# Experts with at most 32 tokens: four 32-column tiles by branch, in a one-core flow-block kernel

## Chip, cores and metric

The kernel runs on one core of a Trainium2 chip. The metric is the device time of one execution in microseconds; before the change it is 1284.41 us (median of 3 runs, 1284.01 to 1285.48).

## What is computed

One block over 256 latent tokens of width 1024 (with 256 context tokens beside them): three token mixers, their merge, and then a mixture of experts, which is what the change touches.

```
def moe_ffn(h, w_router, b_router, w_gate_up, b_gate_up, w_down, b_down):
    logits = (h @ w_router + b_router).astype(jnp.float32)
    top_val, top_idx = lax.top_k(logits, TOP_K)              # 4 of 32
    probs = jax.nn.softmax(top_val, axis=-1)
    combine = jnp.einsum('nk,nke->en', probs, jax.nn.one_hot(top_idx, N_EXPERTS, ...))
    def expert(acc, xs):
        wgu, bgu, wd, bd, cw = xs                            # 1024x2048, 1024x1024
        gate, up = jnp.split(h @ wgu + bgu, 2, axis=-1)
        gate = jnp.minimum(gate, SWIGLU_LIMIT)
        up = jnp.clip(up, -SWIGLU_LIMIT, SWIGLU_LIMIT)
        glu = gate * jax.nn.sigmoid(SWIGLU_ALPHA * gate)
        return acc + cw[:, None] * (((up + 1) * glu) @ wd + bd), None
```

All is float32. The routing gives the 32 experts, in order, 17, 34, 33, 47, 48, 4, 19, 77, 8, 46, 101, 48, 28, 12, 11, 40, 25, 1, 46, 42, 36, 8, 28, 31, 44, 14, 21, 64, 12, 39, 32 and 8 tokens for the inputs used here.

## The kernel before

The mixers, the merge and the routing take the first 310 us. Then a loop in Python (line 1479 on) lays out the 32 experts one after another; the text calls them 0 to 31. The loop is unrolled: every expert has its own instructions on every engine.

**Tokens.** For an expert, `select` (L1358) makes a 0/1 table of its first 64 tokens (`SLOTS`), and `gather` (L1362) turns it into `hT`, the tokens' columns with the features on the 128 partitions, by matmuls against the normalized tokens `h2`; ScalarE applies scale and shift. Gathering is done for two experts at a time.

**Matmuls.** The weights are the moving operand. `gate_up` (L1388, matmul at L1392) loads 64 token columns of `hT` as the stationary operand and streams 512 weight columns past them; two such tiles (q = 0 and 1) stand side by side in the array, each with its own 512 of the 1024 columns, and write the upper and lower 64 partitions of one PSUM bank. Each matmul is float32 and runs as two passes, so the trace shows two records for each. An expert has a first half of `gate_up` (8 steps of 128 features), a second one, and `down` (L1410, matmul at L1414) of the same size. `biases` (L1385) opens each bank with one matmul that puts the bias there.

**Between them.** `act` (L1395) is the clamped SwiGLU on VectorE with one sigmoid on ScalarE. `turn` (L1403) transposes its result on TensorE and copies it to `gT`, the stationary operand of `down`. `spots` (L1373) makes the weighted scatter table, `spread` (L1416) multiplies the output of `down` by routing weight and gate, and `scatter` (L1421) adds it to four PSUM banks by 8 matmuls; an expert's `scatter` is issued within the next expert, after that one's first `gate_up`.

**More than 64 tokens.** Two `tc.If(tv > SLOTS)` per expert (L1503 and L1518) hold `rest_gate` (L1429) and `rest` (L1446), which do tokens 64 to 127 of the same expert with the same weights. TensorE, VectorE and ScalarE each load the expert's count into a register and take the branch by themselves. Experts 7 and 10 enter it. A last `tc.If` (L1557) for over 128 tokens is passed over.

**Weights.** SyncE issues all weight transfers from one list in the order of use (`pump`, L148; the transfer at L161). An expert has six of 2 MB: four for `gate_up` (two per half) and two for `down`; the last expert's `down` comes in four of 1 MB. Nine buffers of 2 MB take them in turn. `done` (key) frees a buffer in the program behind its last reader and issues the next transfer in the list, which waits on the chip until that reader has run.

**Order.** The order of instructions is that of the Python text (a manual schedule); there is no planner.

Of the kernel before, what the change touches and what calls it, by code (L numbers as in the profile page):

```python
# [16 lines left out]
AF = mybir.ActivationFunctionType  # L17
ALU = mybir.AluOpType
# [99 lines left out]
def kernel(ctx, tc, x, cx, cols, rows, csts, wsm, wgt, bada, brt, sgub, bdn, bgu,  # L118
# [45 lines left out]
    def weight(key):  # L164
        if key not in loaded:
            pump()
        return loaded[key][0]
# [6 lines left out]
    def halves(*key):  # L174

        w = weight(key)
        return [w[:, 0:2048], w[:, 2048:4096]]
# [47 lines left out]
    with ExitStack() as p1:  # L225
# [1058 lines left out]
        bsel = Buf(A2, NE, 2)  # L1284
# [20 lines left out]
        G.memset(bsel[:], 0.0)  # L1305
        for r in range(4):
            S.copy(out=bsel[32 * r:32 * r + 32, :, r % 2], in_=ident[32 * r:32 * r + 32, 32 * r:32 * r + 32])
# [15 lines left out]
    def sps2():  # L1323
        sbank.append(sbank.pop(0))
        return sbank[-1]
# [15 lines left out]
    for t in range(2):  # L1341
        mm(ps[0:1, 64:64 + NE], ones[:, 0:1], sel[:, t], start=t == 0, stop=t == 1)

# [10 lines left out]
    sw = ysum[:, 0:256].rearrange("p (t a n) -> p t a n", t=2, a=2)  # L1354
# [18 lines left out]
    def spots(b, sl, e):  # L1373
        for t in range(2):
            V.tensor_scalar_mul(sw[:, t], sl[:, t, :].unsqueeze(1).to_broadcast([P, 2, SLOTS]), cw[:, t, e:e + 1])
        pw = sps2()
        for t in range(2):
            T.transpose(pw[:, P * t:P * t + P], sw[:, t].rearrange("p a n -> p (a n)"), ident[:])  # L1378
        V.tensor_scalar(out=b["sT"][:], in0=pw[:, 0:256], scalar1=0.0, scalar2=None, op0=ALU.is_gt)  # L1379
        V.reduce_sum(out=b["cwv"][:, 0:1], in_=pw[:, 0:256], axis=AX.X)  # L1380

    def bias_of(e):
        V.tensor_copy(out=bse[e % 2][:].rearrange("p (q n) -> p q n", q=2), in_=bsel[:, e, :].unsqueeze(2).to_broadcast([P, 2, SLOTS]))  # L1383
# [11 lines left out]
    def act(b, hf, pg):  # L1395
        gc = b["gc"][hf]
        V.tensor_scalar_min(gc[:], pg[:, 0:256], LIMIT)  # L1397
        S.activation(out=sg[:], in_=gc[:], func=AF.Sigmoid, scale=SW_ALPHA)  # L1398
        V.tensor_scalar(out=up[:], in0=pg[:, 256:512], scalar1=LIMIT, scalar2=-LIMIT, op0=ALU.min, op1=ALU.max)
        V.tensor_tensor(out=gc[:], in0=gc[:], in1=sg[:], op=ALU.mult)  # L1400
        V.scalar_tensor_tensor(out=gc[:], in0=up[:], scalar=1.0, in1=gc[:], op0=ALU.add, op1=ALU.mult)

    def turn(b, hf):  # L1403
        pt = sps2()
        for j in range(2):
# [4 lines left out]
    def down(b, py, ks, w):  # L1410
        for k in ks:
            wk = w[k // 2].rearrange("p (k n) -> p k n", k=2)
            for q in range(2):
                mm(py[64 * q:64 * q + 64, :], b["gT"][:, k, :], wk[:, k % 2, 512 * q:512 * q + 512], start=k == 0, stop=k == KB - 1)  # L1414

    def spread(b, py):  # L1416
        V.scalar_tensor_tensor(out=ysum[:], in0=py[:], scalar=b["cwv"][:, 0:1], in1=g2q[:], op0=ALU.mult, op1=ALU.mult)  # L1417
        S.copy(out=yhx[:], in_=ysum[:])  # L1418
        V.tensor_tensor(out=ylx[:], in0=ysum[:], in1=yhx[:].bitcast(F32), op=ALU.subtract)
# [9 lines left out]
    def rest_gate(e, w):  # L1429

        gather(over, 0, 1)
        gather(over, 1, 1)
        pg = sps2()
        biases(e, 0, pg)
# [11 lines left out]
    def rest(e, g, wu, wd, end=False):  # L1446
        turn(over, 0)
        biases(e, 1, g)
# [19 lines left out]
    biases(0, 0, gbank[0])  # L1468
    V.tensor_copy(out=cnt[:, 0:NE], in_=ps[0:1, 64:64 + NE])
    V.reduce_max(out=cnt[:, NE:NE + 1], in_=ps[0:1, 64:64 + NE], axis=AX.X)  # L1470
    V.tensor_tensor(out=e4[:], in0=m8[:, :, 0:4], in1=m8[:, :, 0:1].to_broadcast([P, 2, 4]), op=ALU.subtract)
# [6 lines left out]
    eq.free()  # L1478
    for e in range(NE):
# [9 lines left out]
        gate_up(hT, g0, range(8), w)  # L1489
        act(cur, 0, g0)  # L1490
        if e:
            scatter(cur)
# [9 lines left out]
        over["hT"] = q_["hT"][:, 4:8].rearrange("p k (i j) n -> p (k i) j n", j=1)  # L1502
        with tc.If(tv > SLOTS):  # L1503
            rest_gate(e, w)
# [9 lines left out]
        if e < NE - 1:  # L1514
            wd = halves("dn", e, 0) + halves("dn", e, 1)
        else:
            wd = [weight(("dn1", e, i)) for i in range(4)]
        with tc.If(tv > SLOTS):  # L1518
            rest(e, g1, wu, wd)
# [9 lines left out]
        turn(cur, 1)  # L1529
        if e + 2 - e % 2 < NE:  # L1530
            gather(q_, e % 2, 2)
        if e + 1 < NE:
            biases(e + 1, 0, g1)
        down(cur, g0, range(4, 8), wd)
        for key in [("dn", e, 1)] if e < NE - 1 else [("dn1", e, 2), ("dn1", e, 3)]:
            done(key)
        if e < NE - 1:
            spread(cur, g0)
        else:
            ylast, lnb = Buf(A, 512), Buf(A, 2, D)  # L1540
            for i in range(2):
                S.dma_start(out=lnb[:, i, :], in_=lnr[2 + i:3 + i, :].to_broadcast([P, D]))
            V.scalar_tensor_tensor(out=ylast[:], in0=g0[:], scalar=cur["cwv"][:, 0:1], in1=g2q[:], op0=ALU.mult, op1=ALU.mult)
            scatter_whole(cur, ylast, True)
# [61 lines left out]
NR2 = 2840  # L1606
NA2S = 2
NA2 = 14592
# [14 lines left out]
def _layout(x, c, ctx, c_ctx, w_ada, b_ada, w_in, b_in, pool_w, pool_scale, qk_conv_w, qk_conv_b, mlstm_norm_g,  # L1623
# [31 lines left out]
    gu = gu.transpose(0, 5, 1, 3, 2, 6, 4, 7).reshape(NE, 4, 2, P, 2048).transpose(0, 1, 3, 2, 4).reshape(NE, 4, P, 4096)  # L1655
    dn = A(w_down)[0].reshape(NE, 2, 4, P, D).transpose(0, 1, 3, 2, 4).reshape(NE, 2, P, 4096)
    bg = A(b_gate_up)[0].reshape(NE, 2, 2, 2, 256).transpose(3, 0, 2, 1, 4).reshape(64, 2, 512)
# [23 lines left out]
```

## Time and profile before

| | |
|---|---|
| median of 3 runs | 1284.41 us |
| the profiled execution, whole | 1286.55 us |
| its span | 1284.7 us |
| mean granted TensorE clock | 0.984 |
| TensorE busy | 1189.9 us (93%) |
| VectorE busy | 461.2 us (36%) |
| ScalarE busy | 284.5 us (22%) |
| read from HBM | 468.92 MB, 366 GB/s over the span |

The whole time is what is compared; the span is the stretch that the profiler's rows cover, and all times in rows count from its start. PE is TensorE's matmuls and PEld its weight loads, which overlap them; a group of matmuls in a row that reads x32 holds 32 records, two for each float32 matmul of the program. Shares over the span mix the first 310 us with the expert loop, so the rows below are from single stretches.

### The profile page before, as it was taken

To read this page: it belongs to the slowest core of one execution; us is meant where nothing else is said; L and a number is where in the kernel's file an instruction comes from. 1 tells how busy PE (TensorE), PEld (TensorE's weight loads), DVE (VectorE), ACT (ScalarE), POOL (GpSimd) and SP (SyncE) were. 2 spreads that over 40 slices of the span, in tenths; PEclk is the share of its full clock that TensorE was granted. 3 is DMA by queue.
4 is the path that set the end of the run, shared out by engine and by line. 5 is a ranking of instruction groups with operands and counts; after the bars stand their busy time and mean duration, and the time that the engine had idled before them with its cause. 6 is when DMAs were issued, how large, how long until landed. Compare 5 with 4: busy or idle time off the path is not lost. (4 is left out here: it accounts for less than half of the span.)

```text
span 1284.7 us, 16504 instructions
## 1 busy us (share of the span) xinstructions
PE 1189.9 (93%) x6619; PEld 611.3 (48%) x6624; DVE 461.2 (36%) x988; ACT 284.5 (22%) x548; POOL 28.3 (2%) x42
## 2 busy tenths in 40 slices
PE   7997999999999999999999999999888999889884
PEld 5897889995333434334433334333333333333321
DVE  6488768796222222222212221222222122212223
ACT  5352745634111111111111111111111111111101
POOL 1000000002000000000000000000000000000000
PEclk9998999998999999999999999999999999999998
DMA  9745648777999999989959999999999999999993
GB/s 389 274 152 204 232 178 296 294 311 297 392 415 427 424 427 427 427 323 429 375 213 387 428 425 427 427 425 427 427 426 426 427 425 427 425 427 426 428 423 149
DMA packets 39470, 471.74 MB, mean 367 GB/s; under 512 B 4529, under 2 KB 4657, under 8 KB 7473
## 3 DMA queue, kind: packets, MB, share of 16 engines
q1 hardware_dynamic: 37008, 463.75, 87.3%
q10 hardware_dynamic: 1696, 4.40, 1.0%
q8 instruction: 89, 1.46, 0.5%
q0 software_dynamic: 640, 1.84, 0.5%
q14 instruction: 37, 0.30, 0.1%
HBM read 468.92 MB, written 1.05 MB: 366 GB/s over the span
## 5 line engine op out<-in xcount | busy, mean ns | idle before, releaser
L1392 PE MATMUL bank<-arena,arena 128*64 128x512 f32 x1808 | 408.8, 596 | 18.3 <-DMA arena<-in_wgu_dram 17.7
L1414 PE MATMUL bank<-arena,arena 128*64 128x512 f32 x1088 | 251.7, 604 | 25.5 <-DMA arena<-in_wdn_dram 17.9
L1392 PEld LDWEIGHTS bank<-arena,arena 128*64 128x64 f32 x1808 | 124.1, 137 | 260.5 <-issue 235.6
L1414 PEld LDWEIGHTS bank<-arena,arena 128*64 128x64 f32 x1088 | 79.3, 138 | 174.8 <-issue 152.7
L246 PE MATMUL bank<-rounded 128*128 128x256 f32 (+1 forms) x1152 | 149.6, 289 | 0.1
L246 PEld LDWEIGHTS bank<-rounded 128*128 128x128 f32 x1152 | 144.0, 195 | 1.8 <-issue 0.6
L1397 DVE TENSOR_SCALAR arena<-bank 128x256 f32<-128x256 f32 x68 | 28.9, 424 | 280.4 <-PE bank L1392 280.4
L1417 DVE SCALAR_TENSOR_TENSOR arena<-bank,arena,g2q 128x512 f32<-128x512 f32 x33 | 24.8, 751 | 271.8 <-PE bank L1414 163.3
L1398 ACT ACTIVATE arena<-arena 128x256 f32<-128x256 f32 x68 | 28.4, 417 | 366.5 <-DVE arena L1397 362.6
L1407 ACT COPY arena<-bank 128x256 f32<-128x256 f32 x68 | 25.3, 372 | 294.4 <-PE bank L1406 294.4
L1392 PE MATMUL bank<-arena 128*64 128x512 f32 x368 | 85.4, 606 | 3.0 <-DMA arena<-in_wgu_dram 2.6
L343 DVE TENSOR_TENSOR rounded<-arena,rounded 128x2048 fp32r<-128x2048 f32 x29 | 66.2, 2284 | 15.1 <-ACT rounded L338 15.1
L1367 PE MATMUL bank<-arena 128*128 128x128 f32 (+1 forms) x576 | 69.9, 275 | 0.7 <-DVE rounded L1383 0.7
L1367 PEld LDWEIGHTS bank<-arena 128*128 128x128 f32 x576 | 66.9, 192 | 1.5 <-ACT arena L1232 0.8
L1370 ACT ACTIVATE arena<-bank,shc 128x128 f32<-128x128 f32 (+1 forms) x144 | 53.3, 450 | 50.7 <-PE bank L1367 50.7
L338 ACT CAST rounded<-arena 128x2048 fp32r<-128x2048 f32 x29 | 55.0, 1898 | 9.2 <-PE bank L246 5.6
L1379 DVE TENSOR_SCALAR rounded<-bank 128x256 fp32r<-128x256 f32 x34 | 14.5, 425 | 117.0 <-PE bank L1378 117.0
L1392 PEld LDWEIGHTS bank<-arena 128*64 128x64 f32 x368 | 25.2, 139 | 53.6 <-issue 45.3
L1418 ACT CAST rounded<-arena 128x512 fp32r<-128x512 f32 x33 | 20.4, 618 | 111.5 <-DVE arena L1417 111.5
L1426 PE MATMUL bank<-rounded 64*128 64x512 f32 x264 | 40.8, 418 | 3.6 <-ACT rounded L1418 3.1
L1426 PEld LDWEIGHTS bank<-rounded 64*128 64x128 f32 x264 | 22.8, 184 | 33.9 <-issue 25.1
L1386 PE MATMUL bank<-rounded 128*128 128x512 f32 x68 | 32.5, 477 | 5.8 <-PEq L1503 3.8
(326 smaller groups left out, 889.5 us busy)
## 6 DMA issues: line engine op xcount, KB each, us to landing
arena<-in_wgu_dram SPq DMA_DIRECT2D x128, 2048.0 KB, 28.7
arena<-in_wdn_dram SPq DMA_DIRECT2D x62, 2048.0 KB, 27.3
arena<-in_win_dram SPq DMA_DIRECT2D x23, 1024.0 KB, 5.3
arena<-in_wada_dram SPq DMA_DIRECT2D x16, 1024.0 KB, 4.9
arena<-in_wad_dram SPq DMA_DIRECT2D x8, 1024.0 KB, 11.1
arena<-in_wbr_dram SPq DMA_DIRECT2D x4, 1024.0 KB, 5.6
arena<-in_wout_dram SPq DMA_DIRECT2D x4, 1024.0 KB, 5.5
arena<-in_wdn_dram SPq DMA_DIRECT2D x4, 1024.0 KB, 33.6
```

Of the source, the lines that this page charges most:

```text
L246: mm(o, l, r, start=start and n == 0, stop=stop and n == len(todo) - 1)
L338: S.copy(out=wh[:, 0:2048], in_=w)
L343: V.tensor_tensor(out=wl[:, 0:2048], in0=w, in1=wh[:, 0:2048].bitcast(F32), op=ALU.subtract)
L1367: mm(pg[:, w * k:w * k + w], h2[:, t, 512 * a + P * k:512 * a + P * k + P], b["sl"][:, t].rearrange("p i n -> p (i n)"), start=t == 0, sto ...
L1370: S.activation(out=b["hT"][:, 4 * a + k].rearrange("p i n -> p (i n)"), in_=pg[:, w * k:w * k + w], func=AF.Identity, scale=shc[:, 1, 4 * ...
L1386: mm(pg[:], bse[e % 2][:], bst[:, hf, :], start=True, stop=False, skip_group_check=True)
L1392: mm(pg[64 * q:64 * q + 64, :], hT[:, k, :], wk[:, k % 2, 512 * q:512 * q + 512], start=False, stop=k == KB - 1, skip_group_check=True)
L1397: V.tensor_scalar_min(gc[:], pg[:, 0:256], LIMIT)
L1398: S.activation(out=sg[:], in_=gc[:], func=AF.Sigmoid, scale=SW_ALPHA)
L1407: S.copy(out=b["gT"][:, 4 * hf:4 * hf + 4, :].rearrange("p (q j) n -> p j q n", q=2), in_=pt[:, 0:256].rearrange("p (j q n) -> p j q n", j ...
L1414: mm(py[64 * q:64 * q + 64, :], b["gT"][:, k, :], wk[:, k % 2, 512 * q:512 * q + 512], start=k == 0, stop=k == KB - 1)
L1426: mm(acc[t][hf][:], b["sT"][sl, P * t:P * t + P], y_[sl, :], start=False, stop=last and y_ is ylx, skip_group_check=True)
```

## The change

Experts 1 to 31 with at most `SMALL` = 32 tokens take a second copy of their code. In it the stationary tile has 32 token columns, four such tiles stand side by side, and each streams 256 weight columns, a quarter of the 1024. `act` then works on 128x128 elements rather than 128x256, `turn` needs one transpose rather than two, and `spread` multiplies the quarter results by a masked gate (`g2m`) and writes them twice, so that `scatter` stays as it is. The columns of the weights are permuted in HBM so that either form finds gate and up columns where it needs them, and the bias goes in by two matmuls (512 and 256 columns; the second table, `bsel2`, is zero for large experts).

The choice is made three times per expert, by `by_count`: a first part (first `gate_up`, `act`, `scatter`, and for the large copy the nested `rest_gate`), a second (second `gate_up`, `spots`, `turn`, `act`, nested `rest`) and a third (`down`, `turn`, `gather` for a later expert, its `biases`, `spread`). Expert 0 has the large copy alone. `done` now stands behind a whole part: the two `down` buffers are freed in the text after the third part. Ahead of the loop come eight small matmuls that put the counts on 128 partitions, four more copies on ScalarE, five VectorE steps and two memsets.

```
...
+    for r in range(4):
+        for t in range(2):
+            mm(ps[32 * r:32 * r + 32, 128:129], sel[:, t], ones[:, 0:1], start=t == 0, stop=t == 1)
...
-    def biases(e, hf, pg):
+    def biases(e, hf, pg, large=False):
         mm(pg[:], bse[e % 2][:], bst[:, hf, :], start=True, stop=False, skip_group_check=True)
+        if not large:
+            mm(pg[:, 0:256], bsb[e % 2][:], bst[:, hf, 256:512], start=False, stop=False, skip_group_check=True)
-    def gate_up(hT, pg, ks, w):
+    def gate_up(hT, pg, ks, w, small=False):
+        n, m = (4, SMALL) if small else (2, SLOTS)
+        c = D // n
         for k in ks:
             wk = w[k // 2].rearrange("p (k n) -> p k n", k=2)
-            for q in range(2):
-                mm(pg[64 * q:64 * q + 64, :], hT[:, k, :], wk[:, k % 2, 512 * q:512 * q + 512], start=False, stop=k == KB - 1,
+            for q in range(n):
+                mm(pg[m * q:m * q + m, 0:c], hT[:, k, 0:m], wk[:, k % 2, c * q:c * q + c], start=False, stop=k == KB - 1,
                    skip_group_check=True)
...
+        def by_count(part):
+
+            if e == 0:
+                part(False)
+                return
+            with tc.If(tv > SMALL) as cmp:
+                part(False)
+            with cmp.Else():
+                part(True)
+
+        def part_a(small):
+            gate_up(hT, g0, range(8), w, small)
+            act(cur, 0, g0, small)
+            if e:
+                scatter(cur)
+            if not small:
+                with tc.If(tv > SLOTS):
+                    rest_gate(e, w)
+
+        def part_b(small):
+            gate_up(hT, g1, range(4), wu, small)
+            spots(cur, p["sl"][:, :, e % 2, :], e, small)
+            turn(cur, 0, small)
+            gate_up(hT, g1, range(4, 8), wu, small)
+            act(cur, 1, g1, small)
+            if not small:
+                with tc.If(tv > SLOTS):
+                    rest(e, g1, wu, wd)
+
+        def part_c(small):
+            down(cur, g0, range(4), wd, small)
+            turn(cur, 1, small)
+            if e + 2 - e % 2 < NE:
+                gather(q_, e % 2, 2)
+            if e + 1 < NE:
+                biases(e + 1, 0, g1)
+            down(cur, g0, range(4, 8), wd, small)
+            spread(cur, g0, small, ylast if e == NE - 1 else None)
+
+        by_count(part_a)
...
         for i in range(2):
             done(("gu", e, i))
-        wu = halves("gu", e, 2) + halves("gu", e, 3)
-        biases(e, 1, g1)
-        gate_up(hT, g1, range(4), wu)
-        spots(cur, p["sl"][:, :, e % 2, :], e)
-        turn(cur, 0)
-        gate_up(hT, g1, range(4, 8), wu)
-        act(cur, 1, g1)
...
-        with tc.If(tv > SLOTS):
-            rest(e, g1, wu, wd)
+        biases(e, 1, g1, e == 0)
+        by_count(part_b)
         for i in range(2, 4):
             done(("gu", e, i))
...
-        down(cur, g0, range(4), wd)
-        for key in [("dn", e, 0)] if e < NE - 1 else [("dn1", e, 0), ("dn1", e, 1)]:
+        by_count(part_c)
+        for key in [("dn", e, i) for i in range(2)] if e < NE - 1 else [("dn1", e, i) for i in range(4)]:
             done(key)
...
-NR2 = 2840
+NR2 = 3096
+SMALL = 32
...
```

How the instructions stand on TensorE now, at two places of expert 1. The first is from the end of the nested `rest_gate` to the second `gate_up`; in the names, `bank_...` is a PSUM bank, `arena_2892` holds `hT` and `gT`, `arena_2574` and `arena` weights, `rounded_2891` the bias and scatter tables, and a form like 64x512 is stationary columns by streamed columns. Before:

```order
L1378 MATMUL bank_98<-ident,arena_2892 128x128 x2
L1392 MATMUL bank_97<-arena,arena_2892 64x512 x4
L1503 UNCONDITIONAL_BRANCH x2
L1386 MATMUL bank_101<-rounded_2891 128x512
L1392 MATMUL bank_101<-arena,arena_2892 64x512 x8
```

And with the change:

```order
L1411 MATMUL bank_97<-arena,arena_2892 64x512 x4
L1551 UNCONDITIONAL_BRANCH x2
L1411 MATMUL bank_99<-arena_2892 32x256 x16
L1411 MATMUL bank_99<-arena,arena_2892 32x256 x16
L1460 MATMUL bank_96<-rounded_2891 128x512 x2
L1460 MATMUL bank_94<-rounded_2891 128x512 x2
L1460 MATMUL bank_100<-rounded_2891 128x512 x2
L1460 MATMUL bank_95<-rounded_2891 128x512 x2
L1540 UNCONDITIONAL_BRANCH
L1401 MATMUL bank_101<-rounded_2891 128x512
L1403 MATMUL bank_101<-rounded_2891 128x256
L1540 COMPARE_AND_BRANCH
```

Behind the large copy with its nested branch stands the small one: 32 matmuls of 32x256 for `gate_up`, and the 8 of `scatter` once more. The bias has a second matmul, and a compare stands ahead of the second part.

The second place is from the end of the second part to `down`. Before:

```order
L1426 MATMUL bank_95<-rounded_2891 128x512 x2
L1518 UNCONDITIONAL_BRANCH x2
L1414 MATMUL bank_99<-arena,arena_2892 64x512 x8
L1406 MATMUL bank_98<-ident,arena_2892 128x128 x2
L1367 MATMUL bank_97<-arena_2892 128x128 x8
L1386 MATMUL bank_101<-rounded_2891 128x512
L1414 MATMUL bank_99<-arena_2574,arena_2892 64x512 x8
```

And with the change:

```order
L1427 MATMUL bank_97<-ident,arena_2892 128x128
L1411 MATMUL bank_101<-arena,arena_2892 32x256 x16
L1540 UNCONDITIONAL_BRANCH
L1540 COMPARE_AND_BRANCH
L1441 MATMUL bank_99<-arena,arena_2892 64x512 x8
L1431 MATMUL bank_98<-ident,arena_2892 128x128 x2
L1377 MATMUL bank_97<-arena_2892 128x128 x8
L1401 MATMUL bank_101<-rounded_2891 128x512
L1403 MATMUL bank_101<-rounded_2891 128x256
L1441 MATMUL bank_99<-arena_2574,arena_2892 64x512 x8
L1540 UNCONDITIONAL_BRANCH
L1441 MATMUL bank_99<-arena,arena_2892 32x256 x16
```

A compare of the count now stands ahead of `down`, and the whole third part, the `gather` for a later expert and the next bias among it, is there twice, once in each copy.

## Rows read from the trace of the kernel before

**Rows 1.** The page's 40 slices: what the DMA engines moved.

```profile
GB/s 389 274 152 204 232 178 296 294 311 297 392 415 427 424 427 427 427 323 429 375 213 387 428 425 427 427 425 427 427 426 426 427 425 427 425 427 426 428 423 149
```

**Rows 2.** Stretches: busy us by engine (x instructions), granted clock, DMA share, GB/s.

```profile
500.00:550.00 50.00, 47.25 (x235) 18.36 (x231) 12.11 (x30) 7.03 (x19) 0.00 (x0) 1.00 1.01 427
550.00:600.00 50.00, 49.38 (x249) 19.57 (x248) 11.14 (x28) 6.98 (x17) 0.00 (x0) 1.00 0.90 361
600.00:650.00 50.00, 49.13 (x250) 20.15 (x248) 11.86 (x31) 7.79 (x21) 0.00 (x0) 1.00 0.87 354
650.00:700.00 50.00, 47.27 (x227) 18.40 (x225) 10.35 (x25) 7.18 (x17) 0.00 (x0) 0.97 0.76 304
```

**Rows 3.** TensorE's timeline in expert 3: start, us, line, form, records [idle before].

```profile
397.19 7.04 PE L1392 MATMUL bank<-arena,arena 128*64 128x512 f32 x32
...
405.52 0.47 PE L1386 MATMUL bank<-rounded 128*128 128x512 f32 x1 [0.17 <-PEq L1503]
405.93 3.65 PE L1392 MATMUL bank<-arena,arena 128*64 128x512 f32 x16
...
423.52 1.03 PE L1392 MATMUL bank<-arena 128*64 128x512 f32 x4
```

**Rows 4.** TensorE's timeline: first stages of experts 21 and 31, and the next wait.

```profile
941.37 2.37 PE L1392 MATMUL bank<-arena,arena 128*64 128x512 f32 x10
...
1239.59 3.65 PE L1392 MATMUL bank<-arena 128*64 128x512 f32 x16 [1.14 <-DMA arena<-in_wgu_dram]
1244.49 1.51 PE L1392 MATMUL bank<-arena,arena 128*64 128x512 f32 x6 [1.25 <-DMA arena<-in_wgu_dram]
```

**Rows 5.** TensorE's timeline: first rows of experts 7, 8, 10 and 11.

```profile
502.57 3.60 PE L1392 MATMUL bank<-arena 128*64 128x512 f32 x16
...
559.66 1.03 PE L1392 MATMUL bank<-arena,arena 128*64 128x512 f32 x4
...
612.38 3.60 PE L1392 MATMUL bank<-arena 128*64 128x512 f32 x16
...
671.14 1.89 PE L1392 MATMUL bank<-arena,arena 128*64 128x512 f32 x8
```

**Rows 6.** SyncE's timeline, expert 7's first weights; the page's DMA issues.

```profile
467.03 0.38 SPq L161 DMA_DIRECT2D arena<-in_wgu_dram  x1
...
arena<-in_wgu_dram SPq DMA_DIRECT2D x128, 2048.0 KB, 28.7
```

**Rows 7.** Line 260: timeline, then its group (ns min/median/max).

```profile
47.53 0.59 PEld L260 LDWEIGHTS bank<-arena 128*32 128x32 f32 x16
47.53 1.07 PE L260 MATMUL bank<-arena 128*32 128x256 f32 x16
...
L260 PEld LDWEIGHTS bank<-arena x128: 106/110/178, 17.0 to 48.0; 128*32 128x32 f32 x128
```

**Rows 8.** TensorE's branch rows of lines 1503 and 1557 (ns min/median/max).

```profile
L1503 PEldq COMPARE_BRANCH  x34: 70/279/357, 316.8 to 1245.4; - x34
...
L1557 PEldq COMPARE_BRANCH  x1: 3752/3752/3752, 1267.3 to 1267.3; - x1
```

**Rows 9.** Timeline around the first `down` of expert 2.

```profile
387.73 2.79 PE L1414 MATMUL bank<-arena,arena 128*64 128x512 f32 x12 [0.31 <-PEq L1518]
...
387.99 0.42 ACT L1398 ACTIVATE arena<-arena 128x256 f32<-128x256 f32 x1 [3.74 <-DVE arena L1397]
```

**Rows 10.** The page: busy time by engine; queue of instruction reads (packets, MB, share).

```profile
PE 1189.9 (93%) x6619; PEld 611.3 (48%) x6624; DVE 461.2 (36%) x988; ACT 284.5 (22%) x548; POOL 28.3 (2%) x42
...
q8 instruction: 89, 1.46, 0.5%
```

**Rows 11.** ScalarE's timeline ahead of the loop.

```profile
307.09 0.90 ACT L1307 COPY arena<-ident 32x32 f32<-32x32 f32 x4
```

**Rows 12.** Stretches in expert 10: TensorE busy, granted clock, DMA share, GB/s.

```profile
655.00:658.00 3.00, 1.58 (x8) 1.00 0.58 246
661.00:664.00 3.00, 3.00 (x12) 0.58 0.00 0
```

More of the change, by code (lines that the diff above doesn't have):

```diff
@@ L1283 @@
         bse = [Buf(R, P) for _ in range(2)]
-        bsel = Buf(A2, NE, 2)
+        bsb = [Buf(R, P) for _ in range(2)]
+        bsel, bsel2 = Buf(A2, NE, 4), Buf(A2, NE, 4)
+        g2m = Buf(A2, 512)
+        few = Buf(A2, 2)
         alid = Buf(A2, P)
@@ L1305 @@
         G.memset(bsel[:], 0.0)
+        G.memset(bsel2[:], 0.0)
+        G.memset(g2m[:], 0.0)
         for r in range(4):
-            S.copy(out=bsel[32 * r:32 * r + 32, :, r % 2], in_=ident[32 * r:32 * r + 32, 32 * r:32 * r + 32])
+            rs = slice(32 * r, 32 * r + 32)
+            S.copy(out=bsel[rs, :, 2 * (r % 2):2 * (r % 2) + 2], in_=ident[rs, rs].unsqueeze(2).to_broadcast([32, NE, 2]))
+            S.copy(out=g2m[rs, 256 * (r % 2):256 * (r % 2) + 256], in_=g2q[rs, 256 * (r % 2):256 * (r % 2) + 256])
         G.tensor_tensor(out=bst[64:128], in0=bgr[64:128], in1=bst[64:128].bitcast(F32), op=ALU.subtract)
@@ L1403, in turn, with act @@
-    def turn(b, hf):
+    def act(b, hf, pg, small=False):
+        j = 1 if small else 2
+        gc, up_, sg_ = (z[:, 0:P * j].rearrange("p (j n) -> p j n", j=j) for z in (b["gc"][hf], up, sg))
+        pj = pg[:, 0:256 * j].rearrange("p (j a n) -> p j a n", j=j, a=2)
+        V.tensor_scalar_min(gc, pj[:, :, 0], LIMIT)
+        S.activation(out=sg_, in_=gc, func=AF.Sigmoid, scale=SW_ALPHA)
+        V.tensor_scalar(out=up_, in0=pj[:, :, 1], scalar1=LIMIT, scalar2=-LIMIT, op0=ALU.min, op1=ALU.max)
+        V.tensor_tensor(out=gc, in0=gc, in1=sg_, op=ALU.mult)
+        V.scalar_tensor_tensor(out=gc, in0=up_, scalar=1.0, in1=gc, op0=ALU.add, op1=ALU.mult)
@@ L1404, in turn @@
+    def turn(b, hf, small=False):
         pt = sps2()
+        if small:
+            T.transpose(pt[:, 0:P], b["gc"][hf][:, 0:P], ident[:])
+            S.copy(out=b["gT"][:, 4 * hf:4 * hf + 4, 0:SMALL], in_=pt[:, 0:P].rearrange("p (r n) -> p r n", r=4))
+            return
         for j in range(2):
@@ L1408, in turn, with down, spread @@
                in_=pt[:, 0:256].rearrange("p (j q n) -> p j q n", j=2, q=2))
-    def down(b, py, ks, w):
+    def down(b, py, ks, w, small=False):
+        n, m = (4, SMALL) if small else (2, SLOTS)
+        c = D // n
         for k in ks:
             wk = w[k // 2].rearrange("p (k n) -> p k n", k=2)
[L1413 to L1417, printed above, removed]
+            for q in range(n):
+                mm(py[m * q:m * q + m, 0:c], b["gT"][:, k, 0:m], wk[:, k % 2, c * q:c * q + c], start=k == 0, stop=k == KB - 1)
+    def spread(b, py, small=False, o=None):
+        y = o or ysum
+        if small:
+            V.scalar_tensor_tensor(out=y[:].rearrange("p (j n) -> p j n", j=2), in0=py[:, None, 0:256].to_broadcast([P, 2, 256]),
+                                   scalar=b["cwv"][:, 0:1], in1=g2m[:].rearrange("p (j n) -> p j n", j=2), op0=ALU.mult, op1=ALU.mult)
+        else:
+            V.scalar_tensor_tensor(out=y[:], in0=py[:], scalar=b["cwv"][:, 0:1], in1=g2q[:], op0=ALU.mult, op1=ALU.mult)
+        if o:
+            return
         S.copy(out=yhx[:], in_=ysum[:])
@@ L1467 @@
     bias_of(0)
-    biases(0, 0, gbank[0])
+    biases(0, 0, gbank[0], True)
     V.tensor_copy(out=cnt[:, 0:NE], in_=ps[0:1, 64:64 + NE])
     V.reduce_max(out=cnt[:, NE:NE + 1], in_=ps[0:1, 64:64 + NE], axis=AX.X)
+    V.tensor_scalar(out=few[:, 0:1], in0=ps[:, 128:129], scalar1=float(SMALL), scalar2=None, op0=ALU.is_le)
+    for q in range(2):
+        V.tensor_scalar_mul(bsel2[:, :, 2 * q + 1], bsel[:, :, 2 * q + 1], few[:, 0:1])
+        V.tensor_tensor(out=bsel[:, :, 2 * q + 1], in0=bsel[:, :, 2 * q + 1], in1=bsel2[:, :, 2 * q + 1], op=ALU.subtract)
     V.tensor_tensor(out=e4[:], in0=m8[:, :, 0:4], in1=m8[:, :, 0:1].to_broadcast([P, 2, 4]), op=ALU.subtract)
@@ L1488 @@
         g0, g1 = gbank if e % 2 == 0 else gbank[::-1]
[L1489 to L1492, printed above, removed]
+        wu = halves("gu", e, 2) + halves("gu", e, 3)
+        if e < NE - 1:
+            wd = halves("dn", e, 0) + halves("dn", e, 1)
+        else:
+            wd = [weight(("dn1", e, i)) for i in range(4)]
+        over["hT"] = q_["hT"][:, 4:8].rearrange("p k (i j) n -> p (k i) j n", j=1)
+        def by_count(part):
+            if e == 0:
+                part(False)
+                return
+            with tc.If(tv > SMALL) as cmp:
[29 more added lines that the diff above has]
+        by_count(part_a)
         if e == NE // 2:
```

53 lines of the change are left out of this document (16 added, 37 removed).

## The prediction

> **What bounds the kernel now.** I read the 40 slices first. From slice 12 on the transfers hold some 427 GB/s in nearly every slice, and sag around 550 to 700 us (323, 375 and 213 in slices 17, 19 and 20) [rows 1], while TensorE is busy 93% of the span [rows 10]. So both look like the bound, and the table of stretches is needed to tell which one is late where. In 500 to 550 us the transfers move 427 GB/s, in 550 to 600, 600 to 650 and 650 to 700 they move 361, 354 and 304 [rows 2]. Counted as idle transfer time that is (66 + 73 + 123) / 427 x 50 = 30.7 us, of which 66 / 427 x 50 = 7.7 lies before 600 us. The rest of the expert loop is carried by the weights: six 2 MB transfers per expert.
>
> Next, one expert on TensorE. Expert 3 runs from 397.19 to 423.52, so 26.33 us: 7.04 us for the first `gate_up`, and four blocks of 16 records at 3.65 (two for the second `gate_up`, two for `down`), together 21.64, and 4.69 of other work [rows 3]. Late in the loop every stage waits for its transfer: from 941.37 (first stage of expert 21) to 1239.59 (expert 31) lie 60 transfers in 298.22 us, 4.97 each, thus 29.8 us per expert [rows 4]. TensorE is therefore quicker than the weights by 3.5 us on an ordinary expert, and time saved on it is worth nothing there. It is the bound in two places only. Expert 7 takes 559.66 - 502.57 = 57.1 us and expert 10 takes 671.14 - 612.38 = 58.8 [rows 5], because they hold over 64 tokens and run the nested branches; buffers come free late, nine of them hold 9 x 4.97 = 44.7 us of transfers, and the stream stops. How long it stops depends on how far TensorE was already behind the weights when it got there. Expert 7's first weights were issued at 467.03 and need 28.7 us [rows 6], so they were there at 495.7, while TensorE began at 502.57: 6.9 us behind, and the idle time is 7.7. For expert 10 the same sum, 6.9 + (612.38 - 502.57) - 18 x 4.97 - 7.7, gives 19.6 us behind, and the idle time is 23.
>
> **The change, step by step.** By the reference's routing 16 of experts 1 to 31 have at most 32 tokens: 5, 6 and 8 before expert 10, and 13 after it. Experts 1 to 4 and 9 take the large path.
>
> *Small matmuls.* A stage has 32 records of 128x512 now (7.04 us) and gets 64 of 128x256. The trace holds that very form in line 260: 16 such records in 1.07 us, with 0.59 us of weight loads inside it [rows 7]. At worst 64 cost 64 / 16 x 1.07 = 4.28 us; without the run-out of a block of 16 nearer 3.5. Three stages: 10.5 to 12.9 us in place of 21.64. To the 4.69 of other work come two 256-column bias matmuls (half of 0.47 each [rows 3]), three jumps of some 0.3 [rows 8], and about 1 us in `part_c`, where half of `down` (now 1.8 us) covers less of the `act` that the next transposes wait for. A small expert takes 18 to 20 us; I take 19.
>
> *Large path.* It pays for the branches. The first `down` used to start at 387.73, while ScalarE's sigmoid of `act` began at 387.99 and takes 0.42 [rows 9]; the next compare now comes after ScalarE has passed the nested branch, so `down` starts some 0.8 us later. With a jump over the small copy (0.3) and two bias matmuls, a large expert costs 1.5 us more, 27.8. Alone that hides behind 29.8 us of weights; not where TensorE is behind, experts 1 to 4 and 9. The overflow experts get this too, and release their third and fourth weight buffers later (in the small copy no such early release exists, so the count must hold on both ways): 59.1 in place of 57.1.
>
> *Expert 7.* Arrival: 4 x 1.5 later, 2 x 7.3 earlier, so 8.6 earlier; but only 6.9 can be used before its weights are there. Idle after: about 2 (it is 2 us longer). Gain 5.7; at small experts of 20 us it is 4.6.
>
> *Expert 10.* Behind by 0 + 59.1 + 19 + 27.8 - 89.5 - 2 = 14.4 to 17 us instead of 19.6; with 2 us more for itself, the gain is 1 to 3. Both together: 5 to 10, and I take **-8 us**. Later small experts save nothing but waiting.
>
> *Instruction reads.* They share the 16 DMA engines with the weights: queue 8 moved 1.46 MB in 89 packets, 0.5% of their time [rows 10], or 6.4 us. TensorE executed 6619 + 6624 instructions, and 30 passed-over nested branches of some 290 instructions were read as well: 21,900 in all, 67 bytes each. The change adds about 113 matmuls per expert to the code, each in two passes with a weight load, 450 instructions; 31 x 450 x 67 B = 0.93 MB, 64% more. By that share 4.1 us, and with the copies on VectorE and ScalarE **+5**. Below: 0.93 MB at 427 GB/s, 2.2. Above: undelayed transfers follow 4.90 us apart (1239.59 to 1244.49 [rows 4]) but average 4.97; were the whole 0.07 due to instruction reads, 64% of 0.07 x 192 is 9. The share is a row about exactly this, so I stay near it.
>
> *Ahead of the loop.* Four more 32-row copies on ScalarE (four took 0.90 [rows 11]) and five small VectorE steps: 0 to 1, taken **+0.7**; the weights run on meanwhile.
>
> *The end.* The last 16 records of `down` take 3.65 us like every such block [rows 3] and become about 2; half of them stand behind the last transfers, so some 1.8 becomes 0.9, and a little goes with the narrower copy before them: **-1.1**. [...]
>
> Sum: -8 + 5 + 0.7 - 1.1 = -3.4 us on the profiled 1286.55, thus 1283.15. That execution lies 2.14 above the median of the three runs, so I predict 1281.0 for the median. A difference under 0.2%, 2.6 us, can't be told from none.
>
> **Rivals.** (a) *Code nearly free:* reads cost 2.2 and experts 7 and 10 give the full 10: 1284.4 - 10 + 2.2 + 0.7 - 1.1 = 1276. For it: the share of queue 8 is small. (b) *All idle time goes:* -30.7 + 5 + 0.7 - 1.1, 1258. Against it: expert 10 needs 59 us and nine buffers hold 44.7. (c) *The code costs the weights more than the stalls give back:* reads at their upper bound of 9 and stalls that shrink by 5: +3.6; with 0.8 us more per branch on large experts, which puts experts 7 and 10 some 4 us later, +7: 1288 to 1291. It decides once a transfer takes over 0.04 us longer than now (8 us / 192). (d) *Jumps miss:* nested branches pass over up to 165 instructions in 0.3 us, but the jump at line 1557, over a whole loop, took 3.75 [rows 8]; the small path must pass over 220 to 245 in `part_a` and `part_b`. At two such jumps a small expert takes 26.5 us, TensorE is 13 behind at expert 7 and 22 at expert 10, idle time is some 39 instead of 30.7, and the sum +13: 1297. [...] (e) *Weight loads of the four tiles don't overlap:* a group of four would take 0.22 + 0.11 us [rows 7], a small expert 22.7, and the gain at expert 7 is eaten by experts 1 to 4: 1289. [...] Rows 7 speak against it: 0.59 us of loads lie inside 1.07. (f) *The small copy isn't taken* (a wrong count): 31 experts at 27.8, TensorE 16 behind at expert 7, idle 43 us, 1302.
>
> **How the numbers follow.** Forecast 0.40, (a) 0.17, (b) 0.05, (c) 0.20, (d) 0.08, (e) 0.06, (f) 0.04. The forecast's own range, 1277 to 1285, splits into 0.22 faster and 0.17 same; faster in all 0.22 + 0.17 + 0.05 = 0.44, same 0.17 + 0.07 (the mild ends of c and e) = 0.24, slower 0.32. The range 1272 to 1292 leaves out b, d and f, 0.17.
>
> **What would show it.** Right: 16 experts with 128x256 records and stages of some 3.5 to 4.3 us; stretches of 500 to 650 us near 427 GB/s and one remaining sag after expert 10 of 20 to 23 us; queue 8 near 2.4 MB; 60 late transfers in about 299.8 us. Wrong: a sag gone altogether (b), branch rows of several us (d), late transfers at 5.02 us or more (c), a small stage over 5 us (e).

## The result, and the profile after

The changed kernel takes 1298.63 us (median of 4 runs, 1296.29 to 1302.12) against 1284.95 before: a ratio of 1.011, 95% interval 1.0094 to 1.0125. It is slower by 13.7 us, where 1281.0 was forecast and the range ended at 1292. The profiled execution took 1296.29, 9.74 more than that of before, and stands at the fast end of the four; what follows accounts for those 9.74.

The page of the changed kernel: its first part, the 40 slices, and the queue of instruction reads.

```profile
span 1294.5 us, 19946 instructions
...
PE 1086.8 (84%) x8206; PEld 626.8 (48%) x8206; DVE 448.0 (35%) x1025; ACT 279.0 (22%) x552; POOL 29.0 (2%) x44
...
GB/s 389 269 158 195 240 175 307 271 347 272 406 425 425 426 423 425 390 349 425 335 227 391 417 425 426 424 426 424 426 425 424 425 426 425 425 426 424 423 405 145
...
q8 instruction: 145, 2.38, 0.7%
```

TensorE has 103 us less to do than in [rows 10], and the time is longer. The sag in the slices is still there [rows 1], and queue 8 has gone from 89 to 145 packets of 16 KB, as forecast. The stretches of [rows 2], in the changed kernel:

```profile
500.00:550.00 50.00, 47.13 (x254) 18.64 (x254) 12.20 (x31) 7.99 (x21) 0.00 (x0) 1.00 0.96 403
550.00:600.00 50.00, 43.68 (x355) 21.67 (x357) 10.20 (x30) 6.56 (x17) 0.00 (x0) 0.97 0.93 375
600.00:650.00 50.00, 46.68 (x234) 19.22 (x232) 10.91 (x29) 7.37 (x20) 0.00 (x0) 0.97 0.83 343
650.00:700.00 50.00, 44.49 (x217) 17.69 (x214) 10.11 (x26) 5.48 (x13) 0.00 (x0) 0.97 0.76 297
```

Idle transfer time is (24 + 52 + 84 + 130) / 427 x 50 = 34 us, 3 more than before, where 8 less were forecast. Nothing was gained at expert 7 or 10: TensorE reaches them at 503.18 and 615.92, later than the 502.57 and 612.38 of [rows 5]. TensorE's timeline from the end of expert 4 over the small experts 5 and 6 to the start of expert 7 tells why (start, us, line, form, records, idle before):

```profile
450.96 3.65 PE L1441 MATMUL bank<-arena,arena 128*64 128x512 f32 x16
457.49 5.35 PE L1411 MATMUL bank<-arena,arena 128*32 128x256 f32 x64 [2.87 <-issue]
...
464.45 1.93 PE L1411 MATMUL bank<-arena,arena 128*32 128x256 f32 x32
...
469.39 1.27 PE L1411 MATMUL bank<-arena 128*32 128x256 f32 x18 [1.54 <-issue]
...
483.11 6.34 PE L1411 MATMUL bank<-arena,arena 128*32 128x256 f32 x64 [5.37 <-issue]
...
503.18 3.65 PE L1411 MATMUL bank<-arena 128*64 128x512 f32 x16
```

The second stages are as short as forecast: 32 records in 1.93 us instead of 16 in 3.65. The first ones are not: 64 records take 5.35 and 6.34 us, over the 5 that the prediction named as a sign of being wrong. TensorE had been idle for 2.87 and 5.37 us ahead of them, and its granted clock was 0.70 and 0.57 in their stretches, a mean of records in the trace that read 1.0 or 0.5. The same 64 records of expert 8, at 565.68, take 3.66 us at 1.00, though TensorE had been idle for 3.38 us ahead of them. The stretches of the three:

```profile
457.40:463.00 5.60, 5.51 (x66) 3.53 (x68) 0.01 (x1) 0.00 (x0) 0.00 (x0) 0.70 1.00 415
483.00:489.50 6.50, 6.39 (x66) 3.32 (x68) 0.00 (x0) 0.00 (x0) 0.00 (x0) 0.57 1.02 431
565.60:569.30 3.70, 3.62 (x66) 2.41 (x66) 0.00 (x0) 0.00 (x0) 0.00 (x0) 1.00 0.95 390
```

Expert 5 lasts from 457.49 to 483.11, 25.6 us, nearly the 26.3 of before. With the wait ahead of it counted, experts 5 and 6 together take from 454.62 to 503.18, 48.6 us, thus 24.3 each. In between TensorE stands idle with no wait that the profile shows ("issue"). The rows of its sequencer at the compares, from all experts (ns min/median/max), and in the page's fifth part the idle time ahead of the `gate_up` matmuls, say the same:

```profile
L1540 PEldq COMPARE_BRANCH  x108: 65/302/6452, 342.3 to 1265.9; - x108
```

```profile
L1411 PE MATMUL bank<-arena,arena 128*32 128x256 f32 (+1 forms) x2640 | 352.7, 503 | 84.2 <-issue 53.3
```

The median compare takes 0.3 us as in [rows 8], the longest 6.45. What the long ones wait for can be read from the starts and lengths of queue 8's packets in the trace. Of the 169 compares behind 340 us 43 take over 1 us, 126 us together, and each of the 43 ends 1.35 to 1.52 us after a packet of code has landed, though the packets follow some 6.4 us apart. The wait amid the matmuls, up to 469.39, ends 1.41 us behind one too. In the kernel before, one compare behind 340 us takes that long, the one at line 1557. So TensorE waits for its code.

Late in the loop the first stages of experts 18 and 31 both wait for their weights:

```profile
858.53 0.65 PE L1411 MATMUL bank<-arena,arena 128*64 128x512 f32 x2 [2.73 <-DMA arena<-in_wgu_dram]
...
1250.92 1.93 PE L1411 MATMUL bank<-arena 128*32 128x256 f32 x32 [1.22 <-DMA arena<-in_wgu_dram]
```

78 transfers in 392.4 us are 5.03 each, against 4.97 in [rows 4]. Expert 31 starts at 1250.92 instead of 1239.59, 11.3 us late, while the span ends only 9.8 later: the end gave back 1.5.

### The profile page after: what moved, and what is told of

It reads as the page before. It is cut to its first block, busy times and chain, and to the rows that moved or that the text cites. A ratio compares the mean times of both kernels' runs of the same rounds, so it can differ in the third digit from the quotient of the medians.

```text
span 1294.5 us, 19946 instructions
## 1 busy us (share of the span) xinstructions
PE 1086.8 (84%) x8206; PEld 626.8 (48%) x8206; DVE 448.0 (35%) x1025; ACT 279.0 (22%) x552; POOL 29.0 (2%) x44
## 5 line engine op out<-in xcount | busy, mean ns | idle before, releaser
L1411 PE MATMUL bank<-arena,arena 128*32 128x256 f32 (+1 forms) x2640 | 352.7, 503 | 84.2 <-issue 53.3
L1411 PEld LDWEIGHTS bank<-arena,arena 128*32 128x32 f32 (+1 forms) x2640 | 133.1, 130 | 271.3 <-issue 230.6
L1441 PE MATMUL bank<-arena,arena 128*32 128x256 f32 (+1 forms) x1600 | 206.1, 478 | 49.1 <-DMA arena<-in_wdn_dram 22.6
L1441 PEld LDWEIGHTS bank<-arena,arena 128*32 128x32 f32 (+1 forms) x1600 | 77.2, 123 | 160.1 <-issue 107.3
L1418 DVE TENSOR_SCALAR arena<-bank 128x256 f32<-128x256 f32 (+1 forms) x68 | 24.6, 362 | 310.6 <-PE bank L1411 310.6
L1419 ACT ACTIVATE arena<-arena 128x256 f32<-128x256 f32 (+1 forms) x68 | 25.0, 368 | 396.4 <-DVE arena L1418 390.2
L1411 PE MATMUL bank<-arena 128*32 128x256 f32 (+1 forms) x560 | 74.2, 502 | 24.5 <-issue 16.0
L1449 DVE SCALAR_TENSOR_TENSOR arena<-bank,arena,g2q 128x512 f32<-128x512 f32 x18 | 13.5, 752 | 157.5 <-PE bank L1441 85.7
L1411 PEld LDWEIGHTS bank<-arena 128*32 128x32 f32 (+1 forms) x560 | 27.2, 129 | 64.4 <-issue 55.1
L1432 ACT COPY arena<-bank 128x256 f32<-128x256 f32 x36 | 13.4, 372 | 169.3 <-PE bank L1431 169.3
L1446 DVE SCALAR_TENSOR_TENSOR arena<-bank,arena 128x512 f32<-128x512 f32 x16 | 12.0, 752 | 107.3 <-issue 61.1
L1460 PE MATMUL bank<-rounded 64*128 64x512 f32 x264 | 44.3, 448 | 3.6 <-ACT rounded L1452 3.1
```

Of the source, the lines that this page charges most:

```text
L1411: mm(pg[m * q:m * q + m, 0:c], hT[:, k, 0:m], wk[:, k % 2, c * q:c * q + c], start=False, stop=k == KB - 1, skip_group_check=True)
L1418: V.tensor_scalar_min(gc, pj[:, :, 0], LIMIT)
L1419: S.activation(out=sg_, in_=gc, func=AF.Sigmoid, scale=SW_ALPHA)
L1441: mm(py[m * q:m * q + m, 0:c], b["gT"][:, k, 0:m], wk[:, k % 2, c * q:c * q + c], start=k == 0, stop=k == KB - 1)
L1460: mm(acc[t][hf][:], b["sT"][sl, P * t:P * t + P], y_[sl, :], start=False, stop=last and y_ is ylx, skip_group_check=True)
```

## The experiments

Two theories stood at first. **R:** the added instructions are read over the same DMA engines as the weights and delay them. **J:** jumps over more than some 200 instructions (an estimate between the 165 and the 220 to 245 of rival (d)) miss code that is at hand, and TensorE waits. The reads were isolated by adding code that never runs.

**dead_late**

```
before.py, in experts 11 to 31, at three places (after scatter, after act, ahead of the second down):
+            with tc.If(tv > 255):
+                for _ in range(2):
+                    gate_up(hT, g0, range(8), w)
+                gate_up(hT, g0, range(2), w)
```

> The kernel before, with three never-taken branches of about 147 TensorE instructions each in experts 11 to 31 (444 more instructions per expert to pass over, nothing more to compute). Theory R (the added instruction reads delay the weights): 9,326 instructions are 0.6 MB or 36 more packets of 16 KB; in the changed kernel the slips between landings cost about 1.55 us per 8.4 packets, 0.18 each, so +6.6 us, about 1291.5, with undelayed landings still 4.89 apart. If the reads cost only their share of 16 engines, as predicted: +2.7, about 1287.5. Theory J (only jumps that miss cost time): the jumps are no longer than those that take 0.3 us now and TensorE has slack from expert 11 on: 1285, no change.

Measured: 1299.66 us, ratio 1.0114 [1.0096, 1.0132], with 125 packets on queue 8. Code that computes nothing costs as much as the whole change. Its transfers alone came nearly to what R had: the last landing is 5.9 us later than before. The rest of the 11.7 us between the two profiled executions was at the end, which neither theory had. TensorE's timeline of the last two experts:

```profile
1245.24 3.65 PE L1414 MATMUL bank<-arena,arena 128*64 128x512 f32 x16 [1.75 <-PEq L1545]
...
1268.67 5.35 PE L1414 MATMUL bank<-arena,arena 128*64 128x512 f32 x16 [2.97 <-PEq L1528]
...
1274.85 3.65 PE L1414 MATMUL bank<-arena,arena 128*64 128x512 f32 x16 [0.46 <-ACT arena L1407]
```

TensorE waits for its own sequencer twice, with weights at hand. Line 1545 is an added branch, whose jump passes over 147 instructions, fewer than the nested branches of before. Line 1528 is the old nested branch for `rest`, right behind an added one: its jump is the same as before, where its compares took 0.43 us at most, and here they take up to 2.92. The block behind that wait takes 5.35 instead of 3.65 us, at a granted clock of 0.56 up to 1272.5 us after the 2.97 us without work (its weight loads come in pairs, 0.85 us apart up to there and 0.43 behind it). So J is wrong as it was put: it isn't the length of a jump.

**unnest**

```
after.py:
         by_count(part_a)
+        with tc.If(tv > SLOTS):
+            rest_gate(e, w)
(and `rest` behind by_count(part_b) in the same way; both taken out of the parts)
```

> The changed kernel with the two branches for over 64 tokens taken out of the large copies and put behind the choice, so that no jump passes over more than 183 instructions (241 and 267 now for the small copy). Theory J: the waits of several us at the compares go, a small expert takes 19 to 20 us, TensorE reaches expert 7 with no delay, the idle time near 560 us goes and the whole is some 8 us shorter, about 1290. Theory R alone: the instruction reads are the same, the time stays at 1296 to 1299.

Measured: 1300.43 us, 1.0127 [1.0098, 1.0156], the same as the changed kernel. The compare of the nested branch, now by itself, in experts 4 to 9, and three of the waits in experts 5 and 6:

```profile
L1584 PEldq COMPARE_BRANCH  x7: 65/2407/6198, 438.8 to 599.9; - x7
```

```profile
465.57 2.49 PE L1411 MATMUL bank<-arena,arena 128*32 128x256 f32 x29 [2.70 <-issue]
...
485.06 0.63 PE L1411 MATMUL bank<-arena,arena 128*32 128x256 f32 x5 [2.38 <-issue]
...
491.37 3.22 PE L1411 MATMUL bank<-arena,arena 128*32 128x256 f32 x26 [3.24 <-issue]
```

The waits have only moved to other places of the code: experts 5 and 6 take from 456.79 to 505.36, the same 48.6 us together as in the changed kernel. J falls.

**late_only and early_only**

```
after.py:
-            if e == 0:
+            if e not in BRANCH:          # range(11, 32) / range(1, 11)
                 part(False)
                 return
```

> The change for experts 11 to 31 alone; experts 1 to 10 as before. Theory R: 40 more packets, +7, and -1.4 at the end, so about 1290.5; the stretch up to 700 us as before (30.7 us idle). Theory J: TensorE has slack from expert 13 on, so its late compares cost nothing: about 1284.

> The change for experts 1 to 10 alone. Theory R: 19 more packets, +3.5. Theory J: experts 5, 6 and 8 wait at their compares, the stops at experts 7 and 10 stay as in the changed kernel, 2 to 4 us longer than before. Both together: +6 to +8, about 1292, and with late_only the two differences add up to that of the whole change (about +13).

Measured: late_only 1291.92 us, 1.0051 [1.0033, 1.0069]; early_only 1288.26, 1.0032 [1.0012, 1.0053]. Both halves cost, late_only about what R said, early_only with 34 us of idle transfers (388, 388, 323 and 318 GB/s in the four stretches). For early_only the 6 to 8 us of the expectation were too much. The two differences, 6.7 and 3.0, come to less than 13.7, though the intervals allow for it.

By now the question was why waits came at any compare. The 36 packets of 16 KB that dead_late added for 9,326 instructions hold 259 each; the estimates below take 256. From 760 to 1240 us queue 8 moved, before and in the changed kernel,

```profile
q8 instruction: 36, 0.59, 0.5%
...
q8 instruction: 66, 1.08, 0.9%
```

which at 29.8 and 30.2 us per expert is some 570 and 1,060 instructions each, run or passed over. (The expectations below count 626, some 50 too many.) That suggested **theory F:** TensorE gets its code block by block, passed over or not, at no less than some 6 us for a block. The shortest distances between packets of queue 8 in the changed kernel's loop were 5.6 to 6.0 us. An expert's 1,060 instructions are 4.1 blocks, thus 25 us. Four kernels tried this.

**dead2_late**

```
dead_late.py:
-        if e >= 11:
+        for _b in range(2 if e >= 11 else 0):
             with tc.If(tv > 255):
```

> As dead_late with twice the never-taken branches (888 more instructions per expert, experts 11 to 31). Theory F (TensorE's instructions come in blocks of 256 at no less than 6 us each, whether they are executed or passed over): an expert's 626 + 888 instructions are 5.9 blocks, 35 to 38 us, more than the 29.8 of its weights, so the instructions become the bound from expert 11 on: 1430 to 1475 us. Theory R (reads only delay the weights, 0.18 us per packet): 73 packets more, +13, with some us more at the end, about 1303.

Measured: 1460.58 us, 1.1361 [1.1315, 1.1408]. Experts 11 and 31 begin in TensorE's timeline at

```profile
670.77 1.46 PE L1392 MATMUL bank<-arena,arena 128*64 128x512 f32 x6
...
1416.80 1.49 PE L1392 MATMUL bank<-arena 128*64 128x512 f32 x6
```

so 37.3 us per expert, in F's range, while the transfers fell to some 340 GB/s. The range was met partly by luck, for the blocks don't follow one another every 6 us here. Of the 111 distances between packets in that stretch 34 are under 4 us (3.2 on average, while the weights move at 195 GB/s in the median) and 41 over 8 (9.5 on average); 6.6 is only the mean of all. An estimate that goes with these distances: 37.3 less the 26.3 us of [rows 3] leaves 11 us for the 888 added instructions, 3.5 blocks, 3.2 each. TensorE's work and its waits for code add up. Its `down` matmuls, grouped (busy us, mean ns, then the idle time ahead of them and who ended it), now wait for the sequencer and no longer for weights:

```profile
L1414 PE MATMUL bank<-arena,arena 128*64 128x512 f32 x1088 | 308.8, 717 | 123.9 <-PEq L1528 65.2 <-PEq L1545 40.2 <-issue 13.7
```

Once added, the dead code cost 14 us; twice, 175. TensorE's code now holds up the loop, and R alone (1303) is far off.

**probe**

```
before.py, behind the second part:
+        for _b in range(16 if e in (10, 20) else 0):
+            with tc.If(tv > 255):
+                for _ in range(3):
+                    gate_up(hT, g1, range(8), wu)
```

> The kernel before with 16 never-taken branches of 193 instructions each behind the second part of expert 10 (where the weights' transfers stand still) and of expert 20 (where they run). Theory F: 12 blocks each; at expert 20 they follow about 6 us apart, some 73 us in all; if the 6 us come from the weights' traffic, those at expert 10 follow closer, down to the 1 us that one packet takes; if the sequencer itself sets them, also 6. Theory R: both pass in 16 x 0.3, some 5 us.

One run, 1348.6 us. At expert 10, with the weights' transfers at a stand, the DMA view from 659 to 695 us shows nothing but code, and its sequencer row the compares:

```profile
DMA packets 12, 0.20 MB, mean 5 GB/s; under 512 B 0, under 2 KB 0, under 8 KB 0
## 3 DMA queue, kind: packets, MB, share of 16 engines
q8 instruction: 12, 0.20, 2.1%
```

```profile
L1521 PEldq COMPARE_BRANCH  x16: 217/2710/3345, 657.9 to 694.4; - x16
```

12 blocks in 36 us, 3.0 to 3.7 from one to the next. At expert 20, from 966 to 995 us, the weights run at some 400 GB/s:

```profile
q1 hardware_dynamic: 798, 11.55, 94.0%
q8 instruction: 5, 0.08, 1.1%
```

5 blocks in 29 us, about 6 from one to the next. Soon after, the weights had filled their buffers and stood still, and the row of the compares from there on shows the pace change in the middle of one and the same run of code:

```profile
L1521 PEldq COMPARE_BRANCH  x10: 219/2897/5437, 991.9 to 1017.8; - x10
```

So in this run a block that is passed over costs 3 us by itself and 6 beside the weights. Of the 16 compares at expert 10 five take 0.2 to 0.3 us, as R had it, and 11 take 2.4 to 3.4, each ending 1.3 to 1.5 us behind a packet of code.

**static3 and static16**

```
after.py:
-            with tc.If(tv > SMALL) as cmp:
-                part(False)
-            with cmp.Else():
-                part(True)
+            part(e in FEW)               # [5, 6, 8] / the 16 small experts
```

These take the routing as known: they are right for these inputs alone.

> Experts 5, 6 and 8 have the small copy alone and all others the large copy alone, without any choice by count (for these inputs the same result). Theory F: with 480 instructions for a small expert nothing is short of code, it takes 19 us; TensorE is at expert 7 before its weights, 12 instead of 20 us behind at expert 10, the idle time falls from 30.7 to about 17, and the time is about 1271. If a small expert is itself slow (weight loads, clock), 24 us or more: 1280 or above.

> As static3 with all 16 experts of at most 32 tokens. Theory F: as static3, 9 packets of instructions fewer (-1.7) and -1.4 at the end: about 1268. If a lower clock in the small experts matters, at or above static3.

Measured: static3 1269.85 us, 0.9881 [0.9864, 0.9897]; static16 1265.27, 0.9852 [0.9834, 0.987]. The same matmuls, without the second copy of the code, gain what the expectations had and more (the large experts are also spared the added jumps). Expert 5 and the start of expert 6 in static3:

```profile
448.85 3.66 PE L1411 MATMUL bank<-arena,arena 128*32 128x256 f32 x64
...
465.13 1.93 PE L1411 MATMUL bank<-arena,arena 128*32 128x256 f32 x32 [0.75 <-DMA arena<-in_wgu_dram]
```

A small expert takes 16.3 us and ends up waiting for weights. The stretches of [rows 2] in static3:

```profile
500.00:550.00 50.00, 47.26 (x241) 19.55 (x237) 10.62 (x28) 6.45 (x18) 0.00 (x0) 1.00 1.01 428
550.00:600.00 50.00, 49.44 (x390) 21.99 (x391) 13.75 (x38) 8.93 (x23) 0.00 (x0) 1.00 1.00 419
600.00:650.00 50.00, 47.26 (x242) 19.61 (x240) 10.96 (x29) 7.12 (x20) 0.00 (x0) 1.00 0.86 355
650.00:700.00 50.00, 49.08 (x239) 18.38 (x236) 13.27 (x35) 6.20 (x16) 0.00 (x0) 1.00 0.95 392
```

Idle transfers: (8 + 72 + 35) / 427 x 50 = 13.5 us instead of 30.7.

**down_early and down_all.** Could a version for any routing gain if its code stays short? The small form went into `down` alone, with one choice per expert and some 770 instructions by the packets of queue 8 (48 from 760 to 1240 us in down_all; the expectation counts 811).

```
before.py, experts 1 to 10 / 1 to 30:
+            with tc.If(tv > SMALL) as cmp:
+                part_c(False)            # down, spots, turn, gather, biases, down, spread
+            with cmp.Else():
+                part_c(True)
```

> The kernel before with the small form for `down` alone, by one choice per expert, in experts 1 to 10 (the scatter table moved into that part); any routing is still computed. Theory F: an expert has 811 instructions, 19 us at 6 us per 256, less than it computes; a small expert takes 23.3 instead of 26.3 us, a large one 0.4 more, TensorE is 4.4 us earlier at expert 7, about 6 us of the 30.7 idle go, 7 more packets cost 1.2: about 5 us faster than before, 1280. If each compare costs a block's wait of 3 to 6 us on TensorE however little code there is: no gain, 1285 to 1290.

> As down_early for experts 1 to 30. Theory F and the price of the reads: the same idle time as down_early, 15 more packets at 0.17 us each, +2.5: about 1282.5.

Measured: 1288.09 us, 1.0027 [1.0017, 1.0038], and 1291.04, 1.0055 [1.004, 1.007]: both a little slower than before. The waits of several us are gone, as F had it. The compares of that choice in experts 3 to 6, and the starts of experts 5 and 6:

```profile
L1555 PEldq COMPARE_BRANCH  x5: 70/213/293, 422.3 to 495.1; - x5
```

```profile
453.14 7.04 PE L1399 MATMUL bank<-arena,arena 128*64 128x512 f32 x32
...
478.55 7.09 PE L1399 MATMUL bank<-arena,arena 128*64 128x512 f32 x32
```

But a small expert still takes 25.4 us (the next one 24.9), not 23.3. Short waits eat the gain: 0.58 us for the sequencer and 0.90 of issue in the first half of `down`, 0.63 ahead of `gather`, whose bank the moved `spots` now uses. The large experts take 27.3 us (371.1, 398.4, 425.8, 453.1), 1 more and not 0.4. TensorE reaches expert 7 at 503.4, no earlier than before, the four stretches move 424, 329, 366 and 292 GB/s (34.8 us idle), and the code reads remain. No version that takes any routing was found to beat the kernel before; one with its spots left in place wasn't tried.

## Why the prediction was wrong

**The step that failed** is the price of a small expert in "Small matmuls": "I take 19". The matmul part of it was right, and even cautious: 64 records in 3.66 us in static3, a whole small expert in 16.3. What it left out is the time until TensorE has its code. The prediction counted all the added code and charged it to the weights, but never asked how fast TensorE can be handed it. Experts 5 and 6 took 24.3 us each, and expert 8, with the wait ahead of it, 22.5 (562.30 to 584.82), against 26.3 before: 8 us were saved on the three, where 22 were forecast. The waits for code, and the lower clock behind two of them, are the difference. At 6 us for each of its 4.1 blocks an expert needs some 25 us, near what was seen. The large experts beside them paid: experts 2 to 4 took 27.7 us instead of 26.3, as forecast (27.8), and expert 9 took 31.1 (584.82 to 615.92) where 27.8 was forecast, with a wait of 2.83 us in it and a granted clock of 0.68 behind that. Expert 7 itself took 59.1 us, as forecast, but TensorE began it at 503.18, 6.9 us behind the landing of its first weights (496.30), just as far behind as before, and it began expert 10 at 615.92, 3.5 later than in [rows 5]. The term of -8 became +3.

**Instruction reads** were the right mechanism, with a term too small: 56 more packets, 0.92 MB, as worked out, but 0.06 us per transfer, some 9 us from expert 7 to the end, and not 5. The lower term came from queue 8's share, which treats 16 engines as one. A transfer's landing stands in the trace as 16 steps of its semaphore. From 760 to 1240 us the first step of the transfers comes every 4.89 us in the kernel before, in the changed one and in dead_late alike; the last step, which TensorE waits for (its three starts of [rows 4] come 0.04 to 0.05 us behind one), comes every 4.97, 5.02 and 5.02. Per packet of code in that stretch the last step falls behind the first by 0.22, 0.20 and 0.19 us. So the delay goes with the packets of code, before the change too, and it meets some of the 16 pieces and not others. Which engine carried which packet the trace doesn't say. The prediction's upper bound of 9, which put the whole of 4.97 against 4.90 down to the reads, was the right one.

**Ahead of the loop** expert 1 began at 342.40, 0.46 us earlier than before (0.7 later was forecast). **The end** gave 1.5 us, where 1.1 was forecast. Sum for the profiled execution: 3 + 9 - 0.5 - 1.5 = 10 of the 9.74 measured.

**The rivals.** (d) gave the right time, 1297, and the right place, waits at compares for code, but the wrong cause of them: with all jumps at 183 instructions or fewer (unnest; the prediction counts 165 for the longest of them) the time was the same, and jumps over 147 waited in dead_late. Its small expert of 26.5 us, its 13 us behind at expert 7 and its idle time of 39 us weren't met (24.3, 6.9 and 34), and its reads of 5 us were 9, so the time came out right partly by luck. What the long compares of the changed kernel have in common is no long jump but a packet of code that lands 1.35 to 1.52 us before they end; what decides is how soon the next packet is there, 3 to 6 us behind the last one as measured. In [rows 3], where a block's worth of instructions takes over 11 us (26.33 for some 570), no such wait shows; it comes where most of a block is passed over. (c) was right that reads cost 9, and its sign, late transfers at 5.02 us or more, came (5.03); it was wrong that the stalls give back anything. (e) fell, though its sign, a small stage over 5 us, came twice: that was the clock, 0.70 and 0.57, and at 1.00 the stage takes 3.66 us, 0.057 per record and 0.23 for a group of four, where (e) had 0.33; 2.41 us of weight loads lie inside its 3.62 of matmuls. (f) fell: 16 experts ran the small form. (a) and (b) fell with reads of 9 us and an idle time that grew. The forecast's sum has no term for a lower clock, though 0.58 stands in [rows 12]. At the end the last 8 records (line 1478) take 3.53 us at a granted clock of 0.55, instead of 1.99, and the 1.5 us that the end gave are net of it. In experts 5 and 6 it cost 1.7 and 2.7 us behind the waits (5.35 and 6.34 against 3.66). A lower mean by itself cost nothing that shows here: static16 is the fastest of all at 0.946.

The range failed because the wait for code was in none of its cases but rival (d), which it left out. The rows before could have given a hint: the kernel had never asked for more than some 570 instructions in 26 us, so they didn't show how fast code can come, and the one place that passed over more, line 1557, waited 3.75 us [rows 8]. The cost should have been bounded from below and above, as that of the reads was.

## What to carry to other kernels

A branch between two unrolled copies wasn't paid by its compare alone here: the code that isn't run is fetched too (36 more packets in dead_late). Divide the instructions of one turn of the loop, run or passed over, by 256, and multiply by the time of a block (measured here: some 6 us beside the weights' transfers at 400 to 425 GB/s, in probe and the changed kernel, and 3 in probe without them): if that comes near the time that the engine should need, the shortcut is lost. It is an estimate of a floor and not the time, for work and waits can add up, as in dead2_late (37.3 us per expert). It is shown for jumps of at most some 270 instructions, about a block. The jump at line 1557 passes over a loop laid out for 32 experts; it took 3.75 us [rows 8], and only two packets of code start behind it in the kernel before, so most of that loop wasn't read. A shortcut is only worth what its own code, its siblings' code and the unfavoured path cost together; to see this before building it, price the copy as code that never runs.

## What the runs showed of the hardware

- Instructions come on queue 8 in packets of 16 KB (16,384 bytes each, 89 before and 145 in the changed kernel). In the changed kernel's loop, from 342 to 1245 us with the weights mostly at some 425 GB/s, successive ones are never under 5.57 us apart (unnest has one distance of 3.1 and one of 4.0); in probe, while nothing else moves, they are 3.0 to 3.7 apart. Each is under way for only about 1 us in either case. What differs is the time until it starts: the packets that end the waits at 452.1 and 476.6 us start 2.7 and 3.9 us after the compare began, those at expert 10 in probe at most 1.0 after it. (Read from the starts and lengths of queue 8's packets and of the compares in the trace.)
- A compare that waits for code ends 1.3 to 1.6 us after a packet has landed: behind 340 us every compare over 1 us does so in the changed kernel (43), unnest (42), dead_late (25), dead2_late (36) and probe (23).
- Code that is never run is not free even where no engine is late: 36 packets moved the last landing by 5.9 us, 0.16 each, four times their bytes at 427 GB/s (0.038). By the 16 steps of each landing it is 0.19 per packet in that run, and 0.19 to 0.22 in before, the changed kernel, unnest, late_only, early_only, static16 and down_all.
- In static16 the granted clock was 0.92 and 0.91 in the stretches from 760 to 1240 us, where TensorE was busy 181 and 179 of 240 us each, against 0.99 and 1.00 before at 224 and 214. The weights set the time there (427 and 423 GB/s), and it cost nothing that shows.
